# Nineteen norm roots moved from ScalarE's Sqrt to one GpSimd power each, in a two-layer gMLP and attention trunk

## The chip, the core and the metric

One core of a Trainium2 chip runs the whole program. The time is device microseconds of one execution, given as the median of three runs; the profile is one further execution of the same kernel, and its instants are microseconds from the start of its span.

## The reference

The input x is (1, 1024, 1024) float32. Layer 0 is a gMLP mixer (Gelu, a LayerNorm over one half of the channels, a causal 128x128 position mixer per channel group), layer 1 a dilated sliding-window attention; each is followed by an MLP with a squared ReLU, and a last RMSNorm ends the program. What matters here are the two norms:

```python
def _rms_norm(x, g):
    y = xf * lax.rsqrt(jnp.mean(xf * xf, axis=-1, keepdims=True) + EPS)
    return (y * g.astype(jnp.float32)).astype(x.dtype)

def _chunk_gating_mixer(h, w_in, ln_g, ln_b, w_s, b_s, w_out):
    uv = jax.nn.gelu(h @ w_in, approximate=False)
    u, v = jnp.split(uv, 2, axis=-1)
    v = _layer_norm(v, ln_g, ln_b)           # the same rsqrt, of the variance
    ...                                      # w_s mixed over each chunk of 128 positions
    return (u * gate) @ w_out
```

## The kernel before

The residual stream `h` lies transposed, channels on the partitions, in 8 tiles of 128x1024, and is worked on in two halves of 512 positions (s = 0, 1). Every product is made of three fp32r products: each operand is split into a high part (ScalarE, L226) and a low part (VectorE, L227, a subtraction with two inputs in SBUF). TensorE's order is written out by hand: a small clock (`Flow`) that counts matmul time sets where side work stands among the matmuls, with waiting times such as `LAT["rms"]` = 2600 ns between a root and its use. A scheduler orders the instructions of the other engines, and chooses which PSUM buffer a tile gets; the tag "at" has five buffers, "mm" three.

An RMSNorm goes like this. `Square.add` squares a tile of `h` on ScalarE (L279) and adds it up on GpSimd (L284), the last on VectorE (L288). `Square.total` multiplies the sums by ones on TensorE, so that a position's sum of squares stands in one PSUM row per position, 128x4 for 512 positions. `rsqrt` makes the root, and `spread` transposes it with a broadcast (L205), so that it lies along the free dimension for all partitions. There are 11 such roots: two of the first norm (into `rs`, shared by the loops below), two for each of the three following norms, and three of the last norm (positions 0 to 511, 512 to 767, 768 to 1023). A LayerNorm root is made per chunk of 128 positions from `bn_stats` and `bn_aggr` (128x1, 8 of them, in `spatial`).

The first stage is the gMLP's v. Three groups of chunks (0 to 2, 3 to 5, 6 and 7) take six PSUM banks, three of each tag, sum over eight weight tiles, and are emptied by ScalarE with Gelu and the scale `rs` (L731, into `vg`). `rs` is thus needed by the first Gelu. Its spread form is evicted by ScalarE into `rsb` (L657) for u. Beside it `gate_weights` sums the position mixer's columns with two matmul pairs (`wsh`, `wsl`, one PSUM bank each, 512 columns), which VectorE adds into `rb` (L683). `spatial` then normalizes a chunk (L704, into `t`), splits it (into `tr`) and multiplies it by the position mixer.

`tc.issue_after(roots[0])` puts the instructions of one weight tile behind the first root, on the engine of that root.

Of the kernel before, what the change touches and what calls it, by code (L numbers as in the profile page):

```python
# [12 lines left out]
F32 = mybir.dt.float32  # L13
F32R = mybir.dt.float32r
AF = mybir.ActivationFunctionType
ALU = mybir.AluOpType
# [3 lines left out]
P = 128  # L20
# [4 lines left out]
EPS = 1e-6  # L25
# [104 lines left out]
def trunk(ctx: ExitStack, tc: tile.TileContext, xT, w_u, w_v, w_o, w_s, b_s, w_qkv, w_vt, w_bo, rel,  # L130
          w_up, w_dn, w_dl, vecs, onehot, outT):
    nc = tc.nc
# [6 lines left out]
    small = ctx.enter_context(tc.tile_pool(name="small", bufs=3))  # L139
# [14 lines left out]
    def slot(shape=(P, S), dtype=F32, name="s"):  # L154

        return slots.tile(list(shape), dtype, tag="s", name=name)
# [54 lines left out]
    make_identity(nc, ident)  # L211
    ones = const.tile([P, P], F32, name="ones")
    nc.vector.memset(ones, 1.0)
    scalars = small.tile([P, 2], F32, name="scalars", bufs=1)
    eps, warm = scalars[:, 0:1], scalars[:, 1:2]
    nc.vector.memset(eps, EPS)
    nc.scalar.activation(warm, eps, AF.Copy)
    h = [slot(name="h") for k in range(KT)]


# [29 lines left out]
    roots = []  # L250

    def rsqrt(src, scale, out=None):

        n = src.shape[1]
        sd = small.tile([P, n], F32, tag="sd", name="sd")
        roots.append(nc.scalar.activation(sd, src, AF.Sqrt, bias=eps, scale=scale).ins)
        v = small.tile([P, n], F32, tag="rv", name="rv")
        nc.vector.tensor_scalar(v, src, scale, EPS, op0=ALU.mult, op1=ALU.add)
        r = small.tile([P, n], F32, tag="rr", name="rr")
        nc.vector.reciprocal(r, sd)  # L260
        a = small.tile([P, n], F32, tag="ra", name="ra")
        nc.vector.tensor_tensor(a, r, v, op=ALU.mult)
        nc.vector.scalar_tensor_tensor(a, a, -0.5, r, op0=ALU.mult, op1=ALU.mult)
        q = small.tile([P, n], F32, tag="rq", name="rq") if out is None else out
        nc.vector.scalar_tensor_tensor(q, a, 1.5, r, op0=ALU.add, op1=ALU.mult)
        return q

    class Square:
# [37 lines left out]
        def rms(self, out=None):  # L306
            with tc.high_priority(offset=PRIO):
                return rsqrt(self.ps[:, 0:self.n // P], 1.0 / D, out)
# [381 lines left out]
    def spatial():  # L690
        for n in range(8):
# [5 lines left out]
            mv = small.tile([P, 2], F32, tag="mv", name="mv")  # L697
            nc.vector.bn_aggr(mv, st.rearrange("p a b -> p (a b)"))
            r = rsqrt(mv[:, 1:2], 1.0)
            parts = []  # L700
            for i in range(2):
# [1255 lines left out]
```

## Time and profile before

| what | us |
|---|---|
| median of 3 runs (lowest to highest) | 2108.82 (2108.45 to 2113.14) |
| the profiled execution: its time, its span | 2107.84, 2106.1 |
| TensorE busy in the span | 2083.1 (99%) |
| VectorE, ScalarE, GpSimd busy | 1572.8, 1183.3, 498.7 |

The profiled execution stands 0.98 us below the median. TensorE is busy nearly all the time at a granted clock of 0.998, so a delay or a gain counts where TensorE waits, and at the two ends of the program. In a timeline row the columns are start, duration, engine, line, operation with output and inputs, shapes and count; what stands in brackets is how long the engine sat idle before it, and what ended that.

### The profile page before, as it was taken

The page shows a single profiled execution, that of the slowest core. Times are in us where ns is not written, and L with a number is a line of the kernel's source. Part 1 is how long each engine was busy: PE and PEld are TensorE (multiplying, and loading weights), DVE is VectorE, ACT ScalarE, POOL GpSimd, SP SyncE. Part 2 cuts the span into 40 slices and gives each one's busy share as a digit, 9 for nine tenths or more (in the row PEclk, how much of TensorE's full clock was granted, in tenths as well). Part 3 has the DMA queues.
Part 4 walks back from the last instruction along what each step waited for, and adds up shares of the span by engine and source line. Part 5 has one row for each costly group of instructions (what it writes and reads, how often), then busy time and mean ns, then how long its engine had stood idle before and what let it go on. Part 6 is the DMA issues. An engine that isn't in the chain of part 4 may idle for free.

```text
span 2106.1 us, 30736 instructions
## 1 busy us (share of the span) xinstructions
PE 2083.1 (99%) x10160; PEld 1720.9 (82%) x10160; DVE 1572.8 (75%) x2902; ACT 1183.3 (56%) x2387; POOL 498.7 (24%) x368
## 2 busy tenths in 40 slices
PE   9999999999999999999999999999999999999998
PEld 7888888888888888888888788888888888888887
DVE  7878759766689998887746666757985446987776
ACT  7645435566675555435556666776556556544432
POOL 3000124323324333430000000002432222433244
PEclk9999999999999999999999999999999999999999
DMA  6428813688766767644865656482256443655432
GB/s 221 130 91 297 308 36 135 200 278 271 261 221 195 230 213 226 233 160 151 307 208 154 184 163 187 156 271 80 91 196 204 146 152 131 203 163 163 141 115 80
DMA packets 224756, 387.10 MB, mean 184 GB/s; under 512 B 39897, under 2 KB 67668, under 8 KB 224596
## 3 DMA queue, kind: packets, MB, share of 16 engines
q1 hardware_dynamic: 215456, 383.77, 55.4%
q10 hardware_dynamic: 9140, 1.36, 0.4%
q8 instruction: 80, 1.31, 0.3%
q14 instruction: 80, 0.66, 0.1%
HBM read 252.24 MB, written 132.81 MB: 183 GB/s over the span
## 4 chain that ended last, share of the span: by engine, by line
PE 84%; DVE 8%; DMA 2%; ACT 2%; issue 2%; POOL 1%; SPq 0%; DVEq 0%; POOLq 0%; ACTq 0%
PE mm L198 42%; PE at L198 40%; PE at L205 2%; DVE y L227 1%; DVE t L227 1%; DVE tr L227 1%; DMA t<-in_w_qkv 1%; DMA h<-in_xT 1%; DVE wp L227 0%; DVE q L1438 0%; DVE r L444 0%; DVE hx L227 0%; DMA r<-in_w_v 0%; POOL t L284 0%; DVE b L449 0%
## 5 line engine op out<-in xcount | busy, mean ns | idle before, releaser
L227 DVE TENSOR_TENSOR wp<-r,wp 128x512 fp32r<-128x512 f32 (+3 forms) x399 | 324.7, 819 | 124.4 <-ACT wp L226 122.1
L226 ACT ACTIVATE wp<-r 128x512 fp32r<-128x512 f32 (+3 forms) x399 | 236.2, 597 | 317.2 <-PE at L198 195.4
L198 PE MATMUL mm<-t,wp 128*128 128x512 f32 x1368 | 344.8, 395 | 0.0
L198 PE MATMUL at<-hx,wp 128*128 128x512 f32 x1452 | 341.0, 389 | 1.7 <-DVE h L1080 1.6
L198 PEld LDWEIGHTS at<-hx,wp 128*128 128x128 f32 x1452 | 272.1, 188 | 60.0 <-DVE h L1080 3.1
L198 PEld LDWEIGHTS mm<-t,wp 128*128 128x128 f32 x1368 | 250.7, 188 | 52.9 <-issue 0.7
L284 POOL TENSOR_TENSOR t<-t 128x512 f32<-128x512 f32 (+1 forms) x60 | 76.8, 1281 | 801.7 <-ACT t L279 799.7
L198 PE MATMUL at<-y,wp 128*128 128x512 f32 x1008 | 245.3, 389 | 0.0
L198 PE MATMUL mm<-hx,wp 128*128 128x512 f32 x984 | 234.3, 389 | 0.0
L198 PEld LDWEIGHTS at<-y,wp 128*128 128x128 f32 x1008 | 189.0, 188 | 39.6 <-issue 0.4
L198 PEld LDWEIGHTS mm<-hx,wp 128*128 128x128 f32 x984 | 184.5, 188 | 38.7 <-DVE hx L227 0.2
L198 PE MATMUL mm<-y,wp 128*128 128x512 f32 x816 | 209.8, 396 | 1.1 <-DVE y L227 0.6
L382 POOL TENSOR_TENSOR t<-r 128x512 f32<-128x512 f32 (+3 forms) x62 | 85.0, 1372 | 476.3 <-DMA r<-in_w_up 146.4
L198 PEld LDWEIGHTS mm<-y,wp 128*128 128x128 f32 x816 | 149.2, 188 | 33.0 <-DVE y L227 1.1
L227 DVE TENSOR_TENSOR hx<-t,hx 128x512 fp32r<-128x512 f32 x192 | 158.7, 831 | 6.1 <-ACT hx L226 5.6
L198 PE MATMUL mm<-y,whi 128*128 128x512 f32 x512 | 158.3, 390 | 1.1 <-DVE t L790 1.1
L198 PE MATMUL at<-t,wp 128*128 128x512 f32 x552 | 130.6, 389 | 0.0
L226 ACT ACTIVATE hx<-t 128x512 fp32r<-128x512 f32 x192 | 119.1, 628 | 19.9 <-DMA t<-hid 16.0
L384 POOL TENSOR_TENSOR r<-r 128x512 f32<-128x512 f32 (+3 forms) x62 | 90.5, 1459 | 165.4 <-DVE wp L227 151.9
L198 PEld LDWEIGHTS at<-t,wp 128*128 128x128 f32 x552 | 103.6, 188 | 21.5
L1080 DVE TENSOR_TENSOR h<-h,at 128x512 f32<-128x512 f32 x144 | 97.8, 680 | 27.6 <-PE at L198 27.1
L198 PEld LDWEIGHTS mm<-y,whi 128*128 128x128 f32 x512 | 95.5, 188 | 21.1 <-issue 1.5
(247 smaller groups left out, 3466.2 us busy)
## 6 DMA issues: line engine op xcount, KB each, us to landing
t<-hid SPq DMA_DIRECT2D x182, 256.0 KB, 4.3
wd<-tr SPq DMA_DIRECT2D x154, 256.0 KB, 3.1
wp<-wd SPq DMA_DIRECT2D x77, 512.0 KB, 4.2
hid<-t SPq DMA_DIRECT2D x140, 256.0 KB, 2.9
r<-in_w_up SPq DMA_DIRECT2D x120, 256.0 KB, 2.8
r<-in_w_dn SPq DMA_DIRECT2D x80, 256.0 KB, 2.7
hid<-b SPq DMA_DIRECT2D x56, 256.0 KB, 2.9
r<-in_w_v SPq DMA_DIRECT2D x48, 256.0 KB, 3.2
```

Source lines behind the costliest of these rows:

```text
L198: nc.tensor.matmul(out, lhsT, rhs, **kw)
L205: nc.tensor.transpose(out, src, ident)
L226: return (nc.scalar.activation(hi, src, AF.Copy).ins, (engine or nc.vector).tensor_tensor(lo, src, hi.bitcast(F32), op=ALU.subtract).ins)
L227: (engine or nc.vector).tensor_tensor(lo, src, hi.bitcast(F32), op=ALU.subtract).ins)
L284: nc.gpsimd.tensor_tensor(self.acc, self.acc, sq, op=ALU.add)
L382: tt(r3, r[0, 0], r[1, 0], op=ALU.subtract)
L384: tt(r[1, 1], r[1, 0], r[0, 0], op=ALU.subtract)
L1080: return engine.tensor_tensor(hs[i, s], hs[i, s], src, op=ALU.add).ins
```

## The change

ScalarE no longer makes roots. Before, a root was a Sqrt on ScalarE (`sd`), a reciprocal (`rr`), and a Newton step of three VectorE instructions with `v` = src * scale + EPS (`ra` twice, then `rq` or `rs`). Now VectorE makes `v` (`rv`) and GpSimd raises it to the power -0.5, with a tile of constants as second operand. The warming activation at the start is a Gelu instead of a Copy. `roots[0]`, behind which one weight tile's instructions were placed, is now an instruction of GpSimd.

```diff
-    scalars = small.tile([P, 2], F32, name="scalars", bufs=1)
-    eps, warm = scalars[:, 0:1], scalars[:, 1:2]
-    nc.vector.memset(eps, EPS)
-    nc.scalar.activation(warm, eps, AF.Copy)
+    power = small.tile([P, 4], F32, name="power", bufs=1)
+    nc.vector.memset(power, -0.5)
+    warm = small.tile([P, 1], F32, name="warm", bufs=1)
+    nc.scalar.activation(warm, power[:, 0:1], AF.Gelu)
...
     def rsqrt(src, scale, out=None):
         n = src.shape[1]
-        sd = small.tile([P, n], F32, tag="sd", name="sd")
-        roots.append(nc.scalar.activation(sd, src, AF.Sqrt, bias=eps, scale=scale).ins)
         v = small.tile([P, n], F32, tag="rv", name="rv")
         nc.vector.tensor_scalar(v, src, scale, EPS, op0=ALU.mult, op1=ALU.add)
-        r = small.tile([P, n], F32, tag="rr", name="rr")
-        nc.vector.reciprocal(r, sd)
-        a = small.tile([P, n], F32, tag="ra", name="ra")
-        nc.vector.tensor_tensor(a, r, v, op=ALU.mult)
-        nc.vector.scalar_tensor_tensor(a, a, -0.5, r, op0=ALU.mult, op1=ALU.mult)
         q = small.tile([P, n], F32, tag="rq", name="rq") if out is None else out
-        nc.vector.scalar_tensor_tensor(q, a, 1.5, r, op0=ALU.add, op1=ALU.mult)
+        roots.append(nc.gpsimd.tensor_tensor(q, v, power[:, 0:n], op=ALU.pow).ins)
         return q
```

The line numbers of the changed kernel are 7 lower behind this function (L284 becomes L277, L731 becomes L724); the power is its L258, `rv` its L256.

The order of TensorE and of the DMA queue is the same instruction for instruction; the other three engines' orders differ around the roots. Three places matter.

ScalarE, from the last squares before the first Gelus to the eviction of `rsb` (`whi` is the high part of a weight, `y` of x, `tr` of a normalized chunk). Before:

```order
L279 ACTIVATE t<-h 128x512 x2
L256 ACT_TABLE_LOAD
L256 ACTIVATE sd<-at,scalars 128x4
L226 ACTIVATE whi<-r 128x512 x2
L731 ACT_TABLE_LOAD
L731 ACTIVATE vg<-at,rs 128x512 x3
L731 ACTIVATE vg<-mm,rs 128x512 x3
L650 ACTIVATE y<-h,vec 128x512
L256 ACT_TABLE_LOAD
L256 ACTIVATE sd<-mv,scalars 128x1
L657 ACTIVATE rsb<-at 128x512
```

And after:

```order
L272 ACTIVATE t<-h 128x512 x2
L226 ACTIVATE whi<-r 128x512 x2
L724 ACTIVATE vg<-at,rs 128x512 x3
L724 ACTIVATE vg<-mm,rs 128x512 x3
L643 ACTIVATE y<-h,vec 128x512
L226 ACTIVATE whi<-r 128x512
L226 ACTIVATE tr<-t 128x512
L650 ACTIVATE rsb<-at 128x512
```

Three table loads and two roots are gone, and `rsb` now stands behind a weight split and behind `tr`, the high part of the first normalized half chunk. (In the whole program 16 table loads become 2: the Gelu's at the start and one for Exp.)

GpSimd, from the affine selects of the gate weights on. Before:

```order
L673 AFFINE_SELECT b<-b 128x512
L284 TENSOR_TENSOR t<-t 128x512 x21
L450 TENSOR_TENSOR keep<-r 128x512
```

And after, down to the first two roots of the second norm:

```order
L666 AFFINE_SELECT b<-b 128x512
L277 TENSOR_TENSOR t<-t 128x512 x6
L258 TENSOR_TENSOR rs<-rv,power 128x4
L258 TENSOR_TENSOR rq<-rv,power 128x1
L277 TENSOR_TENSOR t<-t 128x512 x2
L258 TENSOR_TENSOR rq<-rv,power 128x1
L277 TENSOR_TENSOR t<-t 128x512
L258 TENSOR_TENSOR rq<-rv,power 128x1
L258 TENSOR_TENSOR rs<-rv,power 128x4
L258 TENSOR_TENSOR rq<-rv,power 128x1 x5
```

The first power stands behind three sums of squares of the first half and three of the second; in the last norm they stand behind 2, 3 and 3 sums.

TensorE, the second of the two gate products (with buffer numbers and with the semaphores that it waits for). Before, it took the bank of the first one, which VectorE frees:

```order
L198 MATMUL at_643<-wsh_217,tr_460 128x512 [waits DVE_49,PE_49]
```

And after, it takes the bank of the spread root, `at_608`, which ScalarE's eviction of `rsb` frees:

```order
L205 MATMUL at_608<-ident_82,rs_222 128x128 [waits Activation_49]
L198 MATMUL at_630<-wsh_218,tr_461 128x512 [waits Activation_49]
```

The instruction stands at the same place in TensorE's order, with another buffer and another engine to wait for: the value of the semaphore that it waits for is that of `rsb`.

## The prediction

> **What bounds the kernel now.** I read the page first, for the share of each engine and the chain that ended last.
>
> ```profile
> span 2106.1 us, 30736 instructions
> PE 2083.1 (99%) x10160; PEld 1720.9 (82%) x10160; DVE 1572.8 (75%) x2902; ACT 1183.3 (56%) x2387; POOL 498.7 (24%) x368
> PE 84%; DVE 8%; DMA 2%; ACT 2%; issue 2%; POOL 1%; SPq 0%; DVEq 0%; POOLq 0%; ACTq 0%
> ```
>
> TensorE leaves 23 us of 2106 unused. No instruction of TensorE is added or taken away, so the change can only act on those 23 us, or add to them. The view of TensorE's waits and the windows say where they are:
>
> ```profile
> PE at L205 <- DVE rq L265: 2.5, 2, 2.3
> PE at L205 <- ACT vg L731: 1.7, 1, 1.7
> PE at L198 <- DVE rb L683: 0.4, 1, 0.4
> ...
> 40.00:45.00 5.00, 3.30 (x17) 2.35 (x16) 4.62 (x12) 4.97 (x8) 1.18 (x1) 1.00 0.33 106
> 45.00:50.00 5.00, 4.63 (x21) 3.50 (x20) 4.78 (x18) 4.97 (x9) 0.00 (x0) 1.00 0.02 6
> 2090.00:2100.00 10.00, 5.99 (x45) 5.09 (x43) 9.68 (x30) 3.51 (x10) 2.69 (x4) 0.86 0.56 210
> ```
>
> Of all roots only three are waited for. Two waits are for the root itself (2.3 us in the last norm, 0.2 us in the second). The third, 1.7 us near 43, is for the first Gelu, which waits for the first root's table loads; 0.4 us follow at 46.77. Elsewhere other work hides the root. So three places carry the forecast: 37 to 50 us, the last norm, and a check that the others stay hidden.
>
> **The first root (37 to 50 us).** ScalarE first, then the instructions on the other engines that meet it.
>
> ```profile
> 37.19 1.14 ACT L279 ACTIVATE t<-h 128x512 f32<-128x512 f32 x2
> 38.35 1.28 ACT L256 ACT_TABLE_LOAD   x1
> 39.65 0.26 ACT L256 ACTIVATE sd<-at,scalars 128x4 f32<-128x4 f32 x1
> 39.81 1.14 ACT L226 ACTIVATE whi<-r 128x512 fp32r<-128x512 f32 x2
> 40.97 1.28 ACT L731 ACT_TABLE_LOAD   x1
> 42.27 1.84 ACT L731 ACTIVATE vg<-at,rs 128x512 f32<-128x512 f32 x3
> 43.99 1.85 ACT L731 ACTIVATE vg<-mm,rs 128x512 f32<-128x512 f32 x3
> 45.71 0.75 ACT L650 ACTIVATE y<-h,vec 128x512 fp32r<-128x512 f32 x1
> 47.97 0.58 ACT L657 ACTIVATE rsb<-at 128x512 f32<-128x512 f32 x1
> 50.90 0.62 ACT L226 ACTIVATE tr<-t 128x512 fp32r<-128x512 f32 x1
> ...
> 36.76 4.42 POOL L284 TENSOR_TENSOR t<-t 128x512 f32<-128x512 f32 x3 [7.69 <-ACT t L279]
> 40.23 0.97 DVE L262 TENSOR_TENSOR ra<-rr,rv 128x4 f32<-128x4 f32 x1
> 41.23 0.16 DVE L263 SCALAR_TENSOR_TENSOR ra<-ra,rr 128x4 f32<-128x4 f32 x1
> 41.31 0.69 DVE L227 TENSOR_TENSOR wlo<-r,whi 128x512 fp32r<-128x512 f32 x1
> 44.89 0.64 DVE L696 BATCH_NORM_STATS2 bn<-vg 128x6 f32<-128x512 f32 x1
> 45.45 0.13 DVE L258 TENSOR_SCALAR rv<-mv 128x1 f32<-128x1 f32 x1
> 50.22 0.54 DVE L704 TENSOR_SCALAR t<-vg,mv,rq 128x512 f32<-128x512 f32 x1
> 46.77 0.47 PE L198 MATMUL at<-wsh,tr 128*128 128x512 f32 x1 [0.37 <-DVE rb L683]
> ```
>
> Removed from ScalarE's path: two table loads of 1.28 and `sd`, 2.8 us; without the power the Gelus could start at 39.5. But the power stands on GpSimd behind three sums that end at 41.18 (36.76 + 4.42). And the tiny `ra` took 0.97 us, to 41.20, where its sibling took 0.16: VectorE instructions with two SBUF inputs wait for a GpSimd instruction to end. The two `wlo` are of that kind and now run between the sums; each can push GpSimd by its 0.69. So the power starts at 41.18 (none ahead), 41.87 (one) or 42.56 (both). I take one, since the sums and the `wlo` alternate.
>
> What a power costs no row shows. Below, it is bounded by additions:
>
> ```profile
> L284 POOL TENSOR_TENSOR t<-t 128x512 f32<-128x512 f32 x52 | 70.9, 1365 | 793.7 <-ACT t L279 792.0
> L284 POOL TENSOR_TENSOR t<-t 128x256 f32<-128x256 f32 x8 | 5.9, 736 | 8.0 <-ACT t L279 7.6
> ```
>
> From 736 and 1365 ns, 256 columns cost about 0.63 and the rest is 0.1; 0.2 with the handing over is the low end for four columns. As the high end of my own case I take 1.3, a whole 512-column addition. I take 0.7 for four columns, the 256-column row, since a power is many steps per column, and 0.5 for one column.
>
> Then `rs` is there at 41.87 + 0.7 = 42.6, and the Gelus start 0.35 later than 42.27: the table loads' gain is spent. Now the bank: the second gate product waits for `rsb`, which stands behind `tr` of chunk 0. With the shift of 0.35: `rv` ends at 45.93, its power at 46.4; VectorE does one more `bn` (0.64, from the 45.53 at which the row shown ends, shifted) until 46.5, then `t` (0.54) to 47.05. ScalarE meanwhile does `y` (from 46.06) and `whi` (0.6) to 47.2, then `tr` (0.62) to 47.8, then `rsb` (0.58) to 48.35. TensorE issues the product at 48.35 instead of 46.77: **+1.6**. With 41.18 and 0.2 the shift is -0.8 and the same steps give 47.3, +0.5; with 42.56 and 1.3 for both powers they give 50.3, +3.5. Queued behind the product are all later matmuls; VectorE's last `rb` instructions wait for it, but `tr` and the following weights are then some us ahead of TensorE's need.
>
> The page "ScalarE: Activation LUTs" of the Trainium skill, section "What ACT_TABLE_LOAD costs", puts a switch at 1283 ns plus 1380 ns of drain; by it the two loads would be worth 5.3 us. The rows decide: the first load ends at 39.63 and `sd` starts at 39.65, so the drain isn't there.
>
> **The roots in the middle.** The other 12 table loads, 16 roots and 64 VectorE instructions go from ScalarE and VectorE at no gain, since TensorE waits for none of them, but for the 0.2 in the second norm: **-0.2**. The price is that the power must fit the slack:
>
> ```profile
> 303.88 0.16 DVE L258 TENSOR_SCALAR rv<-at 128x4 f32<-128x4 f32 x1 [1.88 <-ACT sd L256]
> 306.96 0.49 PE L205 MATMUL at<-ident,rq 128*128 128x128 f32 x3
> ...
> 1457.13 5.39 POOL L284 TENSOR_TENSOR t<-t 128x512 f32<-128x512 f32 x4 [3.70 <-ACT t L279]
> 1464.10 0.38 PE L205 MATMUL at<-ident,rq 128*128 128x128 f32 x2
> ```
>
> At 304 the root has 2.9 us from the end of `rv` to its use, and 0.3 more since `rv` no longer waits for `sd`; the other roots of the middle have the same distance by the hand-written order. The tightest is 1464: there the power stands behind four sums that end at 1462.52 and has 1.6. A power of 0.7 fits everywhere: 0.
>
> **The last norm.** Its third root ends on the path.
>
> ```profile
> 2095.66 0.26 ACT L256 ACTIVATE sd<-at,scalars 128x2 f32<-128x2 f32 x1 [0.98 <-PE at L198]
> 2095.96 0.16 DVE L258 TENSOR_SCALAR rv<-at 128x2 f32<-128x2 f32 x1 [0.32 <-ACT sd L256]
> 2097.67 0.16 DVE L265 SCALAR_TENSOR_TENSOR rq<-ra,rr 128x2 f32<-128x2 f32 x1
> 2097.98 0.66 PE L205 MATMUL at<-ident,rq 128*128 128x128 f32 x2 [2.35 <-DVE rq L265]
> 2097.74 4.66 DVE L1878 SCALAR_TENSOR_TENSOR t<-h,vec,at 128x512 f32<-128x512 f32 x11
> ```
>
> The root would be there at about 2096.5 instead of 2097.83. TensorE's 2.35 us of waiting are no loss now, though: VectorE is full of `t` instructions throughout (9.68 of 10 us) and sets the end. So the gain is VectorE's: 0.32 of waiting for `sd`, and four small instructions that each add 0.07 to the next start (2097.67 to 2097.74), 0.28 together: 0.6. The second root takes the same four off and another 0.3 of waiting, but behind it VectorE waits for TensorE's last banks. Ends 0.6 and 1.4; I take 0.7, near the low end for that reason: **-0.7**.
>
> **Sum.** +1.6 - 0.2 - 0.7 = +0.7 us on the profiled execution's 2107.84, 2108.5; that execution lies 0.98 under the median of the runs, so 2109.5. The ends of this case: +0.5 - 0.2 - 1.4 = -1.1 and +3.5 - 0.6 = +2.9, so 2107.7 to 2111.7.
>
> **Rivals.** *A slow power.* If GpSimd works the power out element by element, four columns may take 5 us and one 1.3. The first root then costs 6.5 (the Gelus shift by 4.6, the chunk's power adds 1.3), six roots of the middle and of the last norm miss their 3.1 us by 1.9 each, 11, and the one at 1464 by 3.4: with the 0.6 at the end +20, 2129. It passes 0.3% (6.3 us) where four columns take about 3.3 us: 4.4 + 1.7 + 6 times 0.2 - 0.8. For it: nothing on GpSimd here does more than one step per element. Against: additions show no cost per instruction worth naming. Between 1.3 and 3.3 us the time is 2111 to 2115, still within.
>
> *A first call that fetches code.* The first power would wait once; the nearest row is that of the loads from HBM (the last below):
>
> ```profile
> 8.73 1.34 POOL L284 TENSOR_TENSOR t<-t 128x512 f32<-128x512 f32 x1 [7.35 <-ACT t L279]
> ...
> DMA to landing us min/median/max: 2.7/2.9/3.7
> ```
>
> The Gelus shift by 3.7 more, +4.4 in all, 2113. GpSimd's first addition took 1.34, no longer than the others (1365 ns on average), which speaks against it. The page "GPSIMD Engine Reference" of the Trainium skill, section 2.1, gives a freshly loaded kernel's first call about 6 us; by it the time would be 2115.5.
>
> *The relief counts.* The roots land early, `rsb` is not late because ScalarE runs ahead, and the waits of 1.7, 0.4 and 0.2 close with 1.4 at the end: -3.7, 2105. Against it: the three sums on GpSimd and the order of `rsb`.
>
> **Chances.** My case 0.58; the relief 0.14; a power of 1.3 to 3.3 us 0.10; the code fetch 0.06; the slow power 0.12. A difference of 0.3% is about what these runs can tell from no change. All but the slow power, half of the fetch and a small rest of the relief lie within it: slower 0.15, same 0.82, faster 0.03. The range from 2104.8 (the relief) to 2117 (just past the fetch) leaves out some 2 in 10.
>
> **What would show it.** The power's rows on GpSimd: 0.2 to 1.3 us, no longer first one. The Gelus at 42 to 43. A wait of the second gate product for `rsb` of about 1.5 us or more. No wait of L205 for the root in the middle. The last root's wait at TensorE shorter by over 1 us while the end moves less. A power of over 2 us, or a gate product that doesn't wait, makes the prediction wrong.

## The result, and the profile after

The changed kernel takes 2111.98 us (median of 20 runs, 2109.77 to 2115.22), the kernel before 2109.11 (20 runs, 2106.31 to 2113.14). The ratio is 1.0014, 95% interval [1.0008, 1.0020]: 2.9 us longer, between 1.7 and 4.2. That is within the 0.3% called no change, and on the slow side of it. The profiled execution took 2111.95 us.

From the page its first line and the busy time of each engine, and from the view that sums TensorE's waits the lines that matter here (what waited for what: us in total, times, longest):

```profile
span 2110.2 us, 30656 instructions
PE 2083.1 (99%) x10160; PEld 1721.1 (82%) x10160; DVE 1567.1 (74%) x2826; ACT 1160.1 (55%) x2354; POOL 509.1 (24%) x387
```

```profile
PE at L198 <- ACT rsb L650: 1.6, 1, 1.6
PE mm L198 <- DVE y L227: 1.5, 1, 1.5
PE mm L198 <- ACT mm L1096: 1.3, 2, 0.8
PE at L205 <- ACT vg L724: 1.1, 1, 1.1
PE at L198 <- DVE y L644: 1.1, 1, 1.1
PE at L205 <- POOL rq L258: 1.0, 1, 1.0
PE at L198 <- ACT whi L226: 0.6, 1, 0.6
PE at L198 <- POOL t L277: 0.6, 1, 0.6
```

TensorE's work is the same, 2083.1 us. VectorE and ScalarE lost 5.7 and 23.2 us of work, and the program got no shorter. The last root is waited for 1.0 us instead of 2.35, and no root of the middle any more. New are the wait for `rsb`, 1.5 us instead of 0.6 for `y` L227, and 0.6 instead of 0.3 for a GpSimd sum. The waits for `mm` L1096, `y` L644 and `whi` go back to reads from HBM that land late (for `y` by way of VectorE and GpSimd, which hold each other up behind the read: 1.77 us instead of 0.75); below they turn out to be chance.

The timeline of the first root, GpSimd first, then VectorE, ScalarE and TensorE (start, duration, instruction; in brackets the idle time before it and what ended it):

```profile
37.34 4.74 POOL L277 TENSOR_TENSOR t<-t 128x512 f32<-128x512 f32 x3 [7.64 <-ACT t L272]
42.04 1.47 POOL L258 TENSOR_TENSOR rs<-rv,power 128x4 f32<-128x4 f32 x1
46.93 0.55 POOL L258 TENSOR_TENSOR rq<-rv,power 128x1 f32<-128x1 f32 x1 [3.43 <-DVE rv L256]
39.47 1.46 DVE L227 TENSOR_TENSOR wlo<-r,whi 128x512 fp32r<-128x512 f32 x1 [0.25 <-ACT whi L226]
40.92 1.71 DVE L227 TENSOR_TENSOR wlo<-r,whi 128x512 fp32r<-128x512 f32 x1
38.82 1.14 ACT L226 ACTIVATE whi<-r 128x512 fp32r<-128x512 f32 x2
43.54 1.84 ACT L724 ACTIVATE vg<-at,rs 128x512 f32<-128x512 f32 x3 [3.58 <-POOL rs L258]
48.10 0.66 ACT L226 ACTIVATE tr<-t 128x512 fp32r<-128x512 f32 x1
48.64 0.61 ACT L650 ACTIVATE rsb<-at 128x512 f32<-128x512 f32 x1
49.30 0.50 PE L198 MATMUL at<-wsh,tr 128*128 128x512 f32 x1 [1.63 <-ACT rsb L650]
```

The chain is the forecast one: sums, power, Gelus, `tr`, `rsb`, gate product. ScalarE, freed of table loads, sits idle for 3.58 us until the power is there. All 19 powers, in two groups (ns shortest/median/longest):

```profile
L258 POOL TENSOR_TENSOR rq<-rv,power x17: 546/909/1397, 46.9 to 2100.6; 128x1 f32<-128x1 f32 x8, 128x4 f32<-128x4 f32 x7, 128x2 f32<-128x2 f32 x2
L258 POOL TENSOR_TENSOR rs<-rv,power x2: 1016/1242/1467, 42.0 to 83.1; 128x4 f32<-128x4 f32 x2
```

### The profile page after: what moved, and what is told of

It is laid out like the page before. It is cut to its first block, busy times and chain, and to the rows that moved or that the text cites. A ratio compares the mean times of both kernels' runs of the same rounds, so it can differ in the third digit from the quotient of the medians.

```text
span 2110.2 us, 30656 instructions
## 1 busy us (share of the span) xinstructions
PE 2083.1 (99%) x10160; PEld 1721.1 (82%) x10160; DVE 1567.1 (74%) x2826; ACT 1160.1 (55%) x2354; POOL 509.1 (24%) x387
## 3 DMA queue, kind: packets, MB, share of 16 engines
q10 hardware_dynamic: 9140, 1.36, 0.4%
## 4 chain that ended last, share of the span: by engine, by line
PE 84%; DVE 7%; DMA 4%; ACT 2%; issue 1%; POOL 1%; SPq 1%; DVEq 0%; ACTq 0%; POOLq 0%
PE mm L198 43%; PE at L198 40%; PE at L205 2%; DVE y L227 1%; POOL t L277 1%; DMA t<-in_w_qkv 1%; DMA r<-in_w_v 1%; DVE tr L227 1%; SPq L187 1%; DVE hx L227 0%; DMA h<-in_xT 0%; DVE wp L227 0%; DVE q L1431 0%; DMA hr<-hid 0%; DMA r<-in_w_vt 0%
## 5 line engine op out<-in xcount | busy, mean ns | idle before, releaser
L227 DVE TENSOR_TENSOR wp<-r,wp 128x512 fp32r<-128x512 f32 (+3 forms) x399 | 326.7, 824 | 126.5 <-ACT wp L226 124.0
L277 POOL TENSOR_TENSOR t<-t 128x512 f32<-128x512 f32 (+1 forms) x60 | 77.7, 1297 | 719.5 <-ACT t L272 603.7
L227 DVE TENSOR_TENSOR hx<-t,hx 128x512 fp32r<-128x512 f32 x192 | 158.8, 832 | 6.3 <-ACT hx L226 6.2
```

The source lines that it names most:

```text
L227: (engine or nc.vector).tensor_tensor(lo, src, hi.bitcast(F32), op=ALU.subtract).ins)
L277: nc.gpsimd.tensor_tensor(self.acc, self.acc, sq, op=ALU.add)
```

## The experiments

All kernels here give TensorE the same 10160 matmuls in the same order, so the start of the same matmul can be subtracted between two traces: that shows where time is lost. It is also needed, since the eleven runs that most kernels below have tell a time from that of the kernel before to some 0.9 parts in 1000 only, 2 us. A number such as 1.0010 [1.0001, 1.0019] is the time as a multiple of that of the kernel before, with its 95% interval. For the first stage one measure recurs: from the start of the three sums on GpSimd (37.34 above) to the second gate product (49.30), **11.96 us** in the changed kernel; before, 36.76 to 46.77, **10.01**.

**The same two kernels once more.**

> The changed kernel once more, unchanged, for a second trace. What belongs to the program repeats within 0.05 us: 11.96 us from the start of the three sums on GpSimd to the second gate product, 1.5 us of waiting at 1489, 0.6 us at 2085 and 1.0 us at the last root. What is chance comes out in another size: the waits for reads in the first 25 us (1.7 us in the first trace) and those between 885 and 930 us (1.9 us longer there than in the kernel before). Time 1.2 to 4 us over the kernel before.

> The kernel before once more, unchanged, for a second trace. What belongs to the program repeats within 0.05 us: 10.0 us from the start of the three sums on GpSimd to the second gate product, keep at 4.6 us on GpSimd near 1479, 0.63 us of waiting at 1489, 2.35 us at the last root. The waits for reads in the first 25 us were the smallest in its first trace of all that were taken: here they should be larger, by 0.4 to 2 us, if they are chance, and the same if they belong to the kernel before.

Measured: the changed kernel 1.0010 [1.0001, 1.0019] of the kernel before; the kernel before one run of 2108.26. The sums and the product in the changed kernel's second trace, and then in the second trace of the kernel before (line numbers are 1 higher in both):

```profile
37.61 4.75 POOL L278 TENSOR_TENSOR t<-t 128x512 f32<-128x512 f32 x3 [8.32 <-ACT t L273]
49.59 0.50 PE L199 MATMUL at<-wsh,tr 128*128 128x512 f32 x1 [0.26 <-ACT rsb L651]
```

```profile
37.08 4.42 POOL L285 TENSOR_TENSOR t<-t 128x512 f32<-128x512 f32 x3 [7.62 <-ACT t L280]
47.09 0.47 PE L199 MATMUL at<-wsh,tr 128*128 128x512 f32 x1 [0.37 <-DVE rb L684]
```

11.98 and 10.01: the first stage costs 1.95 us, and both numbers repeat to 0.02. How late TensorE's instructions start against the first trace of before, in us, taken from the four traces:

| TensorE's instruction (its start in the first trace of before) | before again | after | after again |
|---|---|---|---|
| first square sums by ones (35.68) | 1.26 | 1.81 | 1.23 |
| second gate product (46.77) | 0.32 | 2.53 | 2.82 |
| a matmul of the MLP (866.33) | 0.01 | 2.42 | 2.80 |
| the same layer's end (925.90) | 0.42 | 4.27 | 3.75 |
| behind the attention (1412.72) | 0.28 | 3.46 | 3.03 |
| the one that waits for `y` (1489.19) | 0.30 | 4.39 | 3.94 |
| ahead of the last norm (2080.90) | 0.45 | 4.48 | 3.98 |
| end of the span (2106.1) | 0.45 | 4.11 | 3.63 |

The 1.2 to 1.8 us of the first line are waits for reads, in a stretch where no root has been made yet; the kernel before has them too, and they are chance (-0.1 to 1.8 in the thirteen traces taken). Most of this lateness goes away again: the kernel before comes in 1.26 late and goes out 0.32 late, since the Gelus and not TensorE set the pace here. Chance too is most of what is lost between 866 and 926 (0 and 0.41 before, 1.85 and 0.95 after, but 2.22 in the next kernel, whose roots are the old ones there, and -0.29 in one with powers). Only 0.2 of it, at 926, comes in every trace with powers in the third norm (0.15 to 0.30) and in no other (0.02 at most).

What repeats with the powers is the first stage (of its 1.95 us 0.15 come back near 55), -0.38 at the first root of the second norm (283.70, between two lines of the table), those 0.2, +0.9 at 1489, and -0.37 and -0.35 from 2080.90 on. Near 1154 both traces of before lose 0.7 us that no other trace loses. It begins at a transfer in the attention (`ex<-sc`), which lands 4.1 us behind its issue in these two and 3.3 to 3.4 in the eleven others, the one with the old roots there among them. Why is not shown.

**Powers in the first stage alone.**

```diff
 def rsqrt(src, scale, out=None):
+    if len(roots) >= 10:
+        ...                      # Sqrt, reciprocal, Newton step as before
```

> The first ten roots (both of the first norm and the eight of the chunks) are powers on GpSimd as in the changed kernel; the nine later ones are the old Sqrt, reciprocal and refinement, with their table loads. Theory A, the first stage holds most of the loss (Gelus late behind three sums, then the second gate product late behind the eviction rsb): the time stays 1.9 to 2.9 us over the kernel before, 2111.0 to 2112.0 where the kernel before has 2109.1; the second gate product waits about 1.6 us for rsb. Rival B, the loss comes from the later roots (GpSimd and VectorE hold each other up near 1480, and in the last norm): at most 0.7 us over before, up to 2109.8. Rival C, the 1.8 us that the trace of the changed kernel lost on the first reads, before any root, belong to the program: the same loss of 1.8 us by 24 us in this trace; by chance it would be another size here.

Measured 1.0007 [0.9998, 1.0016], 1.4 us over: between A's 1.9 and B's 0.7, so the time doesn't decide. The stages do. The first one takes 11.99 us (37.58 to 49.57); at 1489 nothing is lost (4.22 late at 1412.72, 4.24 at 1489.19) and in the last norm nothing is won (4.34, 4.31). So theory A holds for the largest part, and B for 0.9 us of it. Rival C is out by the table above: the early waits for reads come and go in traces of one kernel.

**The first root old, the others powers.**

```diff
 def rsqrt(src, scale, out=None):
+    if not roots:
+        ...                      # Sqrt, reciprocal, Newton step as before
```

> Only the very first root is the old one (Sqrt, reciprocal, refinement, with its table load, and the Gelu table loaded again behind it); the other 18 are powers. Theory A: the Gelus start as before, near 42.3, not 1.3 later; the chunk's power and tr still stand ahead of rsb, so the second gate product is late by about 1.2 us instead of 1.95: 0.7 to 0.8 us under the changed kernel, 2111.2 where before has 2109.1. If the first root's own place is all of the loss, 2109.5. Rival B (later roots): 2112, as the changed kernel.

Measured 0.9999 [0.9990, 1.0008], under the 2.1 us over the kernel before that I expected. Its sums and its product:

```profile
37.06 4.41 POOL L292 TENSOR_TENSOR t<-t 128x512 f32<-128x512 f32 x3 [6.79 <-ACT t L287]
47.67 0.47 PE L198 MATMUL at<-wsh,tr 128*128 128x512 f32 x1 [0.96 <-DVE rb L691]
```

10.61 us: of the 1.95, 1.35 are gone and 0.6 are left, where I had expected 1.2 to be left. But here the scheduler gives the product another bank, which VectorE's `rb` frees and not `rsb`, so the 1.35 are the first root's place and the bank together; this kernel doesn't tell them apart.

**`rsb` ahead of `tr`.**

```diff
-        nc.scalar.activation(rsb[:, half(s)], pb, AF.Copy)
+        with tc.high_priority(offset=PRIO):
+            nc.scalar.activation(rsb[:, half(s)], pb, AF.Copy)
```

> As the changed kernel, but ScalarE's eviction rsb stands ahead of the first chunk's tr instead of behind it. Theory A (the second gate product waits for rsb's bank): the product starts about 0.55 us sooner, its wait falls from 1.6 to about 1.1 us, and the time from 2112.0 to 2111.4. Rival B: the time stays, since the product's wait only takes the place of a later one; the trace then shows the wait shorter and another longer by the same.

Measured 1.0004 [0.9996, 1.0013]. The sums, `rsb` and the product:

```profile
36.27 4.73 POOL L277 TENSOR_TENSOR t<-t 128x512 f32<-128x512 f32 x3 [7.15 <-ACT t L272]
47.03 0.62 ACT L651 ACTIVATE rsb<-at 128x512 f32<-128x512 f32 x1
47.70 0.50 PE L198 MATMUL at<-wsh,tr 128*128 128x512 f32 x1 [1.13 <-ACT rsb L651]
```

11.43 us, 0.53 less, the wait 1.13: here as in the changed kernel the product starts 0.05 us behind the end of `rsb`. The bank is shown to be the cause of this wait. What is won is kept, against rival B: TensorE is 0.94 us late at the product and 0.83 at 59 us.

**The root ahead of the sums.** In the first kernel `rv` also goes ahead of the `wlo`; the second leaves VectorE's order alone and has `rsb` first.

```diff
+            elif k < KT - 1 and self.held is not None:
+                self.held.append(sq)      # the second half's sums wait
...
+                    if gi == 0:
+                        with tc.issue_after(roots[0]):
+                            sq[1].release()
```

> As the changed kernel, but the first power stands ahead of the three sums of the second half on GpSimd, and its rv ahead of the wlo on VectorE. Theory A: rv at about 38.8, the power from 39.0 to 40.0, the Gelus at 40.0 instead of 43.5, rsb about 3 us sooner; TensorE's waits for the first Gelu (1.1) and for rsb (1.6) close or nearly so: 2.5 to 4 us under the changed kernel, 2108.0 to 2109.5 where it has 2112.0. This is the rival of the prediction in which the relief counts, made to happen. Rival B (the loss comes from later roots): within 0.7 us of the changed kernel, 2111.3 to 2112.7, the waits only moving to a later place.

> As the changed kernel, but the three sums of the second half stand behind the first power on GpSimd, and rsb ahead of the first chunk's tr on ScalarE; VectorE keeps the order of the changed kernel (rv behind one wlo, and the wlo that TensorE needs not pushed back as in the run early_root_rv). Theory A: the Gelus start about 1.8 us sooner than in the changed kernel, the second gate product 2.3 us sooner (about 9.6 us behind the point at which the square of the third tile ends, against 11.96 there and 10.01 in the kernel before); the time comes to within 0.5 us of the kernel before, some 2.3 us under the changed kernel. Rival: what is won at the product is lost again a few us later, as in early_root_rv, and the time stays where the changed kernel's is.

Measured 1.0005 [0.9996, 1.0014] and 1.0001 [0.9993, 1.0010]. In the first, the power, the first Gelus, and what TensorE met behind the product; then the stretches around 50 us (length; busy time of TensorE, its weight loads, VectorE, ScalarE and GpSimd; granted clock; share of the DMA engines; GB/s):

```profile
38.74 1.40 POOL L258 TENSOR_TENSOR rs<-rv,power 128x4 f32<-128x4 f32 x1 [9.40 <-DVE rv L256]
40.17 1.84 ACT L733 ACTIVATE vg<-at,rs 128x512 f32<-128x512 f32 x3 [0.80 <-POOL rs L258]
50.30 0.72 PE L198 MATMUL at<-wlo,y 128*128 128x512 f32 x1 [2.24 <-DVE wlo L227]
```

```profile
48.00:50.00 2.00, 0.06 (x1) 0.00 (x0) 2.00 (x6) 2.00 (x5) 0.07 (x1) 1.00 0.00 0
50.00:52.00 2.00, 1.70 (x4) 1.43 (x5) 2.00 (x3) 1.44 (x3) 1.92 (x2) 0.60 0.35 101
52.00:54.00 2.00, 2.00 (x6) 1.54 (x6) 2.00 (x2) 0.14 (x1) 1.07 (x1) 0.54 0.11 38
```

The Gelus come at 40.17, as expected, and the product is 1.16 us earlier than in the kernel before. But the time is 1.1 us over that of the kernel before, where I expected 0.4 over at most: VectorE now does the gate's `rb` and `tr` ahead of a `wlo` that TensorE needs. TensorE waits 2.24 us for it, and then runs at a granted clock of about half for some 3.5 us. From 59 us on it is 2.75 us late: against the changed kernel 3.7 are won at the product (2.53 + 1.16), and 3.9 lost behind it (1.16 + 2.75). In the second kernel:

```profile
39.00 1.14 ACT L226 ACTIVATE whi<-r 128x512 fp32r<-128x512 f32 x2
40.49 1.40 POOL L258 TENSOR_TENSOR rs<-rv,power 128x4 f32<-128x4 f32 x1 [10.57 <-DVE rv L256]
47.17 0.50 PE L198 MATMUL at<-wsh,tr 128*128 128x512 f32 x1 [1.11 <-ACT rsb L660]
```

From the `whi` to the product 8.17 us, against 10.48 in the changed kernel (38.82 to 49.30): 2.31 less, 2.3 expected, and it is kept (0.41 us late at the product, 0.40 at 59). In time this kernel is 1.2 us under the changed kernel of the same session, which the scatter doesn't tell from the 2.3. The three kernels told next are built on this one and show 8.16 or 8.17 too. So the first stage's loss was the order on GpSimd and ScalarE, and can be taken back: 11.96 - 2.31 is 9.65, 0.36 less than the 10.01 of the kernel before.

**The later roots near 1464 and 1473.** All three are the kernel just told, but with one or two old roots: those that meet the condition `len(roots) == 15`, `== 14` or `in (14, 15)`.

> As early_rsb, and the root near 1473 us alone is the old one (Sqrt, reciprocal, refinement). Theory: that power is what makes VectorE and GpSimd take turns near 1480, so that keep takes 4.6 us on GpSimd again, the two y 0.69 each, and the 0.9 us that TensorE waits longer at 1489 is gone: 0.9 us under early_rsb, about 1 us under the kernel before. Rival: the turns near 1480 come from another root or from the drift of the phases, and the wait at 1489 stays 1.5 us.

> As early_rsb, and of the two roots near 1464 and 1473 us only the earlier is the old one. In early_rsb_mix the later alone was old, and TensorE still waited 0.9 us longer at 1489. Theory: the earlier root decides (with it old, VectorE runs later into the stretch and doesn't stop before r at 1480, so GpSimd's keep takes 4.6 us and the y 0.69 each): the wait at 1489 is 0.6 us, 0.9 us under early_rsb. Rival: it takes both, and the wait stays 1.5 us. About the kernel before's time, 0.5 us either way.

> As early_rsb, and both roots near 1464 and 1473 us are old. Both theories: the stretch near 1480 is that of the kernel before, keep 4.6 us, the wait at 1489 0.6 us; if it isn't, the turns near 1480 hang on the phase in which the kernel arrives and not on the roots. By the stages, against the kernel before: first stage -0.8 to +0.4, the second norm -0.2, 1489 0, last norm -0.35: 0.2 to 1.3 us faster.

Measured 1.0004 [0.9995, 1.0013], 1.0005 [0.9995, 1.0014] and 0.9999 [0.9990, 1.0007]: none can be told from the kernel before. GpSimd and VectorE near 1480, in the kernel before (with what TensorE waits for there), after, with the earlier root old, and with both old:

```profile
1479.19 4.63 POOL L450 TENSOR_TENSOR keep<-r 128x512 f32<-128x512 f32 x1 [13.46 <-ACT y L226]
1478.97 1.29 DVE L227 TENSOR_TENSOR y<-r,y 128x512 fp32r<-128x512 f32 x2
1477.05 1.40 DVE L444 SCALAR_TENSOR_TENSOR r<-h,vec,at 128x512 f32<-128x512 f32 x2
PE mm L198 <- DVE y L227: 0.6, 1, 0.6
```

```profile
1482.43 1.62 POOL L443 TENSOR_TENSOR keep<-r 128x512 f32<-128x512 f32 x1 [4.46 <-ACT y L226]
1482.22 2.38 DVE L227 TENSOR_TENSOR y<-r,y 128x512 fp32r<-128x512 f32 x2
1480.29 1.41 DVE L437 SCALAR_TENSOR_TENSOR r<-h,vec,at 128x512 f32<-128x512 f32 x2 [0.61 <-PE at L205]
```

```profile
1479.45 1.63 POOL L466 TENSOR_TENSOR keep<-r 128x512 f32<-128x512 f32 x1 [4.46 <-ACT y L228]
1477.31 1.41 DVE L460 SCALAR_TENSOR_TENSOR r<-h,vec,at 128x512 f32<-128x512 f32 x2 [0.62 <-PE at L205]
```

```profile
1479.21 4.64 POOL L466 TENSOR_TENSOR keep<-r 128x512 f32<-128x512 f32 x1 [13.48 <-ACT y L228]
1477.08 1.40 DVE L460 SCALAR_TENSOR_TENSOR r<-h,vec,at 128x512 f32<-128x512 f32 x2
```

In the kernel before, `keep` takes 4.6 us, some three of them held up, while six VectorE instructions pass in a row at about 0.69 us each, the two `y` first, to 1482.67 (each has two inputs in SBUF, and `keep` reads SBUF). After, `keep` gets its turn at once and the second `y` takes 1.1 us longer beside it; the turns go on, and TensorE, which waits for `y` (1.5 us instead of 0.6), loses 0.9. One old root doesn't undo this (0.91 lost in the first kernel, 0.90 in the second, between 1412.72 and 1489.19), both do (0.01): my theory of the one root is wrong, twice. In each of the nine traces that lose, VectorE sat idle ahead of `r` (0.61 to 0.97 us, for L205); in none of the four that don't. As I read it, with fewer small instructions VectorE catches up with TensorE and stops; no run varies this alone. Why GpSimd has its turns after such a stop, though `keep` comes 0.2 us behind the first `y` in both cases, isn't shown.

**Each power twice.**

```diff
+        twice = small.tile([P, n], F32, tag="rr", name="rr")
+        nc.gpsimd.tensor_tensor(twice, v, power[:, 0:n], op=ALU.pow)
         roots.append(nc.gpsimd.tensor_tensor(q, v, power[:, 0:n], op=ALU.pow).ins)
```

> Every power is done twice on GpSimd, the result of the first is not used. Theory A: the first root's Gelus start 1.0 us later than in the changed kernel and the chunk's root 0.55, so the second gate product 1.5 us later; the root near 1467 misses its use by 0.4 us; the sums of the last norm stand 1.0 us later at 2085: in all 2 to 3 us over the changed kernel, 4.5 to 6 over the kernel before. The other roots have 3 us and hide it. Rival: GpSimd's share of the port counts everywhere, and VectorE's starts slip at every norm: more than 5 us over the changed kernel.

Measured 1.0034 [1.0021, 1.0046], 7.2 us over the kernel before, and 2115.75 against 2111.81 for the changed kernel in the same session: 3.9 over it, where 2 to 3 were expected. By the stages: the sums start at 36.81 and the product at 50.24, 13.43 us, 1.47 over the changed kernel (1.5 expected); 1.36 instead of 0.93 lost up to 1489, 0.4 more, as expected; but the last norm, from 2080.90 to the end, loses 1.44 where the changed kernel wins 0.37, 1.8 instead of 1.0, and there the expectation fell short. The rival is out: between 46.77 and 866.33, with a whole norm in it, nothing is lost (3.47 late, then 3.13). The last norm in the changed kernel, GpSimd and then the two waits of TensorE:

```profile
2085.94 1.54 POOL L277 TENSOR_TENSOR t<-t 128x256 f32<-128x256 f32 x2 [1.67 <-ACT t L272]
2087.43 1.02 POOL L258 TENSOR_TENSOR rq<-rv,power 128x4 f32<-128x4 f32 x1
2088.42 1.54 POOL L277 TENSOR_TENSOR t<-t 128x256 f32<-128x256 f32 x2
2090.02 0.61 PE L198 MATMUL at<-ones,t 128*128 128x1 f32 x4 [0.60 <-POOL t L277]
2101.35 0.69 PE L205 MATMUL at<-ident,rq 128*128 128x128 f32 x2 [1.04 <-POOL rq L258]
```

The power stands ahead of two sums of the next positions, and these end on TensorE's path: it waits for them 0.60 us at 2090.02, where it did not wait before, and 1.59 with two powers.

## Why the prediction was right, and where not

**The first root: right in kind, 0.35 us short.** 1.6 forecast, 1.95 measured, within 0.5 to 3.5. All links were there: the queue behind the sums, VectorE's two `wlo` and the sums holding each other up (1.46 and 1.71 us instead of 0.69, the sums 4.74 instead of 4.42), the bank, `rsb` behind `tr`, a wait of 1.63. The power started 4.70 us behind the sums' start, where I had 5.11 (41.87 - 36.76); the second `wlo` ends at 42.63, inside the power's own time. The power was mis-sized: 1.47 us for 0.7, over my high end of 1.3. So the Gelus came 6.20 us behind the sums' start instead of 5.51 in the kernel before, 0.69 later and not 0.35. That they start at 43.54 and not at 42 to 43, a sign that failed, is this and the 0.58 by which the sums started later, which is chance.

**The price of a power.** One column took 0.55 us (0.5 taken), two 0.71, four 1.02 (0.7 taken): about 0.16 more a column. Beside VectorE instructions with two inputs four columns took 1.4. The slow power and its time of 2129 are out. A first call that fetches code is out: the very first power takes 1.40 where no sum stands ahead of it, and the sixteenth, near 1476, takes 1.40 too. The 6 us that the Trainium skill gives for it ("GPSIMD Engine Reference", section 2.1) are shown by no run here.

**The middle: the step that failed** is "at no gain, since TensorE waits for none of them", with the slack of the power as the only price. The powers fit; but I took freed VectorE time for harmless. With the two old roots near 1464 and 1473 gone, VectorE and GpSimd take turns at 1480, and that costs 0.9 us. The gain at the second norm I took half too small, from the view of TensorE's waits. The root's line in the kernel before:

```profile
283.70 0.65 PE L205 MATMUL at<-ident,rq 128*128 128x128 f32 x4 [0.17 <-DVE rq L265]
```

The view counts the 0.17 in which TensorE stood idle. But the matmuls stand 0.23 us apart here, and this one starts 0.55 behind the one ahead of it; in the changed kernel that distance is 0.22. So 0.38 is won with the four matmuls of the line together, in each of the ten traces with powers there; the three others, with the old root, differ by 0.00.

**The last norm: right in kind, half the size.** -0.36 for -0.7, and outside its ends of -0.6 and -1.4. The last wait shrank by 1.3 us (2.35 to 1.04) while the end moved less, as forecast. Left out was that the first of the three powers queues ahead of the next sums and costs 0.77 at the instruction behind them, which the gain at the last root had to pay.

**The sum.** +0.7 was forecast; by the stages it is 1.8 - 0.38 + 0.2 + 0.92 - 0.36 = 2.2 (1.5, if the 0.7 near 1154 are the change's), and the runs say 2.9 [1.7, 4.2] and, the second time, 2.1 [0.2, 4.0]. The first is the upper end of my own case (+2.9). It lies well inside the whole range, which at 12 us is wide, so that says little. The relief did not come in this order, but its mechanism is real: with the root ahead of the sums, the wait for the first Gelu is 0 to 0.75 us in five traces, against 1.13 and 2.00 in the changed kernel.

**The profile I started from** was a lucky one: of thirteen traces only one other reached the first norm as early, and at 22 us none did. The 1.7 us of waiting for the first Gelu, which the relief counted on, hang on that too: in the second trace of the same kernel they are 0.83. One trace cannot show that; a second does.

## What to carry to other kernels

Moving a small operation to an idle engine moves it into that engine's queue: price it by what stands ahead of it (4.7 us of sums here) and by what then stands behind it, not by its own microsecond. Removing instructions from an engine off the path is not free either where it shares a resource with another: look at who runs beside it. And where a difference is smaller than the scatter, compare the same instruction of the engine that bounds, stage by stage, over two traces of each kernel; the first stage, the loss at 1489 and the gain in the last norm repeated to 0.02 us when the totals scattered by 5.

No version here beats the kernel before measurably; the best two, with the first root ahead of the sums and late roots old, and with the first root alone old, are at 0.9999 of it.

## What the runs showed of the hardware

TensorE's granted clock fell to half behind some waits of about 2 us. In the changed kernel's second trace (busy time of TensorE, its weight loads, VectorE, ScalarE and GpSimd, granted clock, share of DMA, GB/s):

```profile
44.00:46.00 2.00, 1.44 (x6) 1.35 (x7) 1.46 (x3) 2.00 (x4) 0.00 (x0) 0.64 0.40 124
46.00:48.00 2.00, 2.00 (x6) 1.55 (x5) 1.93 (x6) 2.00 (x5) 0.55 (x1) 0.51 0.00 0
```

It had waited 2.00 us for the first Gelu; then half speed cost some 1.5 us by my estimate, and the wait for `rsb` took up most of that (0.26 instead of 1.63). Waits of 2.24 and 2.22 did the same in two other traces; of 1.95, 1.79 and, at 611, 2.12 us not. At the end of the changed kernel the wait was only 1.04 us, behind sixteen matmuls of one column, and the clock fell too (0.72 from 2100 to 2102, then 0.50). So the length of the wait alone doesn't decide. The Trainium skill ("TensorE: Matmul & The Clock Gate", "What's actually happening") has the clock halved after an idle window of some 3.4 us; here 2.0 us were enough, and not always.

A GpSimd instruction can be held up for several VectorE instructions in a row (`keep`, 4.63 us for 1.3 to 1.6, with six of them passing). The Trainium skill ("SBUF — State Buffer", "SBUF: two separate sides") says only that whoever starts first holds the shared port to the end, and not who comes next.
